# A chunked state-space scan on one core: broadcast decays and exponentials loaded per chunk, tanh written over the taps' input

## The chip, the core and the metric

The kernel runs on one core of one Trainium2 chip. The metric is the device time of one execution in microseconds (us); the median of three executions of the kernel before is 2815.06 us.

## What is computed

Two pre-norm residual layers run over 1024 tokens of width 1024, batch 1, in float32: a mixer of mLSTM and retention heads, an MLP, a second mixer (Mamba-2 SSD) and another MLP. The change touches the second mixer alone. It has 32 heads of 64 in 8 groups of 4, state size 128, a causal depthwise convolution of 4 taps, and chunks of 128 tokens. What it computes, cut to what matters here:

```python
zxbcdt = u @ w_in
z, xbc, dt = jnp.split(zxbcdt, (SSD_INNER, SSD_INNER + SSD_CONV_DIM), axis=-1)
xbc = jax.nn.silu(causal_depthwise_conv(xbc, conv_w, conv_b).astype(F32))
xs, bm, cm = jnp.split(xbc, (SSD_INNER, SSD_INNER + SSD_GROUPS * SSD_STATE), axis=-1)
dt = jax.nn.softplus(dt.astype(F32) + dt_bias.astype(F32))
cs = jnp.cumsum(dt * a.reshape(ng, rep), axis=2)            # inside a chunk
seg = jnp.exp(jnp.where(mask, cs[:, :, :, None] - cs[:, :, None, :], -jnp.inf))
cb = jnp.einsum('bctgn,bcsgn->bctsg', cm, bm)
m = cb[..., None] * seg * dt[:, :, None]
y_intra = jnp.einsum('bctsgr,bcsgrp->bctgrp', m, x)
states = jnp.einsum('bclgn,bclgr,bclgrp->bcgrpn', bm, to_end, x)
h_c = exp(cs[:, :, -1]) * h_{c-1} + states                  # from chunk to chunk
y_inter = jnp.einsum('bctgn,bcgrpn->bctgrp', cm, h_prev) * jnp.exp(cs)[..., None]
y = y_intra + y_inter + d_skip * xs
yg = y * silu(z);  yg = group_rmsnorm(yg) * norm_w;  out = yg @ w_out
```

## The kernel before, in words

Tokens lie along the free dimension and channels on the partitions; a half is 512 tokens. Every float32 weight is split into a high and a low part (`split`, L92 to L95: ScalarE writes `whi`, VectorE subtracts to get `wlo`), and a projection of 128 columns for one half (`proj_in`, L136) is 24 matmuls of 512 columns into one PSUM bank.

The second mixer (`ssd`) goes over 8 groups of heads. First `ssd_dt` computes the cumulated log-decays and their exponentials for all tokens and stores them in DRAM as `cs_d` and `ecs_d`, one row per head. In each group then:

- **Projection and taps.** Four column blocks (B, C and two of x) are projected, 2 halves each. ScalarE copies the PSUM bank into `xr` (L769) and writes the last tap into `sact` (L770), VectorE adds three more taps (L774), ScalarE takes the tanh (L778, into a tile `th`), and VectorE finishes the SiLU (L779).
- **Scan.** 8 chunks, 4 in each half. For each half `cbp` (L801) is the product of B and C, masked into `cb`. For each chunk the log-decays of the group's four heads, 4 x 128 numbers, are loaded from `cs_d` and broadcast over 128 partitions into `cb4` (L812, 256 KB written; the profile calls the tile `cb`). ScalarE makes the decay matrix of them: four Relu instructions, one per head (L816), and one Exp (L823). VectorE multiplies by `cb` (L824). TensorE transposes x and B (`tr`, L829); VectorE scales x into `xd` and `xw` (L832, L852), ScalarE copies the transposed B into `bn` (L856). TensorE computes the chunk's own part and the part from the state, both into one PSUM tile `yp` (L838, L843), and the new state's contribution `ds_` (L858), which needs `bn` and `xw`. VectorE adds it to the state, which GpSimd has multiplied by the chunk's decay. The part from the state is multiplied by the broadcast exponentials `eh` (L872) and added (L883). `eh` is loaded per half, for 4 heads by 64 partitions each, in 4 transfers of 128 KB (L793).
- **Gate and output.** Two column blocks of z are projected (L136), gated and squared (L893 to L909); a matmul with ones, `sp` (L914), sums the squares; the output projection (L180) follows.

The program's text is written in this order, but a scheduler sets the order on each engine: it interleaves the z projection's 96 matmuls with the scan's small steps, and moves instructions ahead where it estimates that their inputs are there. Each engine runs its queue strictly in order. Of the z matmuls stand, between the `tr` of a chunk and its `yp`, in the second group and the ones after it: before 18, 4, 10, 10, 9, 8, 16 and 9 for chunks 0 to 7, 4 between `yp` and `ds_` of chunk 0, and 8 after the last chunk. Loads are all issued by the SP queue. `cb4` has 2 buffers before, so that the load of chunk c+2 waits for the matmuls L838 of chunk c; the loads for the next group's first two chunks are issued in the scan of this one.

Of the kernel before, what the change touches and what calls it, by code (L numbers as in the profile page):

```python
# [7 lines left out]
F32 = mybir.dt.float32  # L8
# [4 lines left out]
P = 128  # L13
# [4 lines left out]
HALF = 512  # L18
# [5 lines left out]
class Trunk:  # L24
# [694 lines left out]
    def ssd(self, w_in, conv_w, conv_b, dt_bias, a_log, d_skip, norm_w, w_out, mask):  # L719
        nc, tc = self.nc, self.tc  # L720
        with ExitStack() as ctx:
            one = ctx.enter_context(tc.tile_pool(name="ss1", bufs=1))
            two = ctx.enter_context(tc.tile_pool(name="ss2", bufs=2))
# [27 lines left out]
            nat, cs_d, ecs_d, dec, by_token = self.ssd_dt(one, w_in, dt_bias, a_log)  # L751


            for g in range(8):
                conv = []
                for j in (2, 3, 0, 1):
                    jt = (g * 2, g * 2 + 1, 16 + g, 24 + g)[j]
                    w = self.split_in(self.load_in(w_in, 2048 + jt * P))
                    outs = []
                    prev = None  # L760
                    for half in range(2):
                        ps = self.proj_in(w, half)
                        t = self.half_tile(half, f"sact{half}")
                        xr = two.tile([P, HALF + 3], F32, name="xr", tag="xr", bufs=3)
                        if half == 0:
                            nc.gpsimd.memset(xr[:, 0:3], 0.0)
                        else:
                            nc.gpsimd.tensor_copy(xr[:, 0:3], prev[:, HALF : HALF + 3])
                        nc.scalar.copy(xr[:, 3 : 3 + HALF], ps)  # L769
                        nc.scalar.activation(  # L770
                            t, ps, AF.Identity, scale=cw[:, 3, jt : jt + 1], bias=cw[:, 4, jt : jt + 1]
                        )
                        for k in range(3):
                            nc.vector.scalar_tensor_tensor(  # L774
                                t, xr[:, k : k + HALF], cw[:, k, jt : jt + 1], t, op0=ALU.mult, op1=ALU.add
                            )
                        th = two.tile([P, HALF], F32, name="th", tag="th", bufs=2)
                        nc.scalar.activation(th, t, AF.Tanh)  # L778
                        nc.vector.scalar_tensor_tensor(t, th, 1.0, t, op0=ALU.add, op1=ALU.mult)  # L779
                        outs.append(t)  # L780
                        prev = xr
                    conv.append(outs)
# [3 lines left out]
                hs = slice(g * 4, g * 4 + 4)  # L786
                state = None
                for half in range(2):
                    o = half * HALF
                    eh = two.tile([P, 2, HALF], F32, name="eh", tag="eh", bufs=1)  # L790
                    for tl in range(2):
                        for j in range(2):
                            nc.sync.dma_start(  # L793
                                eh[j * 64 : (j + 1) * 64, tl],
                                ecs_d[g * 4 + tl * 2 + j, o : o + HALF].partition_broadcast(64),
                            )

                    cbp = self.sc.tile([P, CPH, P], F32, name="cbp", tag="sc")
                    for cc in range(CPH):
                        s = slice(cc * P, (cc + 1) * P)  # L800
# [5 lines left out]
                    y = (x0[half], x1[half])  # L806
                    for cc in range(CPH):
                        c = half * CPH + cc
                        s = slice(cc * P, (cc + 1) * P)
                        par, q = c % 2, c // 2  # L810
                        cb4 = two.tile([P, 4, P], F32, name="cb4", tag="cb4", bufs=2)
                        nc.sync.dma_start(  # L812
                            cb4, cs_d[hs, c * P : (c + 1) * P].partition_broadcast(P)
                        )
                        for h in range(4):
                            nc.scalar.activation(  # L816
                                cb4[:, h],
                                cb4[:, h],
                                AF.Relu,
                                scale=-1.0,  # L820
                                bias=nat[:, 2, par, g * 4 + h, q : q + 1],
                            )
                        nc.scalar.activation(cb4, cb4, AF.Exp, scale=-1.0)  # L823
                        nc.vector.tensor_mul(  # L824
                            cb4, cb4, cb[:, cc].unsqueeze(1).broadcast_to([P, 4, P])
                        )
                        tr = self.sc.tile([P, 4, P], F32, name="tr", tag="sc")
                        for j, src in enumerate((x0, x1, bT)):
                            nc.tensor.transpose(tr[:, j], src[half][:, s], self.ident)  # L829
                        xn = tr[:, 0:2].rearrange("p a (h d) -> p (a h) d", h=2)  # L830
                        xd = two.tile([P, 4, 64], F32, name="xd", tag="xd")
                        nc.vector.tensor_mul(  # L832
                            xd, xn, nat[:, 0, par, hs, q : q + 1].broadcast_to([P, 4, 64])
                        )
                        yp = self.sc.tile([P, 4, P], F32, name="yp", tag="sc")
                        for h in range(4):
                            r = slice((h % 2) * 64, (h % 2) * 64 + 64)
                            nc.tensor.matmul(  # L838
                                yp[r, h // 2], xd[:, h], cb4[:, h], start=True, stop=True
                            )  # L840
                        if c > 0:
                            for tl in range(2):
                                nc.tensor.matmul(  # L843
                                    yp[:, 2 + tl],
                                    state[:, tl * P : (tl + 1) * P],
                                    cT[half][:, s],
                                    start=True,
                                    stop=True,
                                )
                        if c < NCH - 1:  # L850
                            xw = two.tile([P, 4, 64], F32, name="xw", tag="xw")
                            nc.vector.tensor_mul(  # L852
                                xw, xn, nat[:, 1, par, hs, q : q + 1].broadcast_to([P, 4, 64])
                            )
                            bn = two.tile([P, P], F32, name="bn", tag="bn")
                            nc.scalar.copy(bn, tr[:, 2])  # L856
                            ds_ = self.sc.tile([P, HALF], F32, name="ds_", tag="sc")
                            nc.tensor.matmul(  # L858
                                ds_[:, 0:256], bn, xw.rearrange("p h d -> p (h d)"), start=True, stop=True
                            )  # L860
                            new = two.tile([P, 256], F32, name="sst", tag="sst")
                            if c == 0:
                                nc.scalar.copy(new, ds_[:, 0:256])
                            else:
                                nc.gpsimd.tensor_mul(
                                    new.rearrange("p (h d) -> p h d", h=4),
                                    state.rearrange("p (h d) -> p h d", h=4),
                                    dec[:, hs, c : c + 1].broadcast_to([P, 4, 64]),
                                )
                                nc.vector.tensor_add(new, new, ds_[:, 0:256])  # L870
                        if c > 0:
                            nc.vector.tensor_mul(eh[:, :, s], eh[:, :, s], yp[:, 2:4])  # L872
                        for tl in range(2):
                            nc.vector.scalar_tensor_tensor(
                                y[tl][:, s],
                                y[tl][:, s],
                                dsk[:, g * 2 + tl : g * 2 + tl + 1],
                                yp[:, tl],
                                op0=ALU.mult,
                                op1=ALU.add,  # L880
                            )
                            if c > 0:
                                nc.vector.tensor_add(y[tl][:, s], y[tl][:, s], eh[:, tl, s])  # L883
                        if c < NCH - 1:
                            state = new
                zs = []
                for j in range(2):
                    w = self.split_in(self.load_in(w_in, g * 256 + j * P))
                    outs = []
                    for half in range(2):  # L890
                        ps = self.proj_in(w, half)
                        t = self.z_tile("sz")
# [5 lines left out]
                for half in range(2):  # L898
                    hid = self.hid_tiles()
                    y = (x0[half], x1[half])  # L900
# [200 lines left out]
```

## Time and profile before

| | |
|---|---|
| median of 3 executions | 2815.06 us (2813.73 to 2817.12) |
| the profiled execution's own time | 2813.8 us |
| its span, first to last instruction | 2812.0 us |
| mean granted TensorE clock | 0.993 of full speed |
| TensorE matmuls (PE) busy | 2735.5 us, 97% |
| VectorE (DVE) busy | 1696.3 us, 60% |
| ScalarE (ACT) busy | 933.9 us, 33% |
| GpSimd (POOL) busy | 500.3 us, 18% |
| chain that ended last, by engine | PE 91%, DMA 4%, ACT 2%, DVE 2%, POOL 1% |

Busy times are of the whole span, which has stages with different limits; the second mixer takes the stretch from about 1203 to 2112 us. Its eight scans lie some 114 us apart. A busy matmul row tells that one was in the engine, not that it ran at its peak. The waiting time of an engine costs only where the engine that bounds the stage is held up in turn. The chain goes back from the last instruction, at each step to what released it.

### The profile page before, as it was taken

The numbers are of one execution on the slowest core, as the hardware profiler recorded it, in microseconds if no ns is written. First come the engines' busy times: TensorE is split into PE (matmuls) and PEld (weight loads), VectorE is DVE, ScalarE is ACT, GpSimd is POOL, SyncE is SP. The second block draws the span as 40 slices with busy tenths as digits, with TensorE's granted clock in tenths as the row PEclk, the third lists the DMA queues.
The fourth block names the chain that finished last, engine by engine and source line by source line (L and its number), as shares of the span: only waits on it lengthen the run. The fifth ranks groups of instructions, "written<-read, shape, count | busy, mean of one in ns | idle before, by whom it ended". The sixth has DMA issues, their size and how long they took to land.

```text
span 2812.0 us, 33165 instructions
## 1 busy us (share of the span) xinstructions
PE 2735.5 (97%) x13149; PEld 2206.2 (78%) x13149; DVE 1696.3 (60%) x2794; ACT 933.9 (33%) x1547; POOL 500.3 (18%) x454
## 2 busy tenths in 40 slices
PE   8999999999999999899999999999999999999997
PEld 7788787888888888687787777777778888888885
DVE  5544436645656445876667667666676566654457
ACT  5131223322222222443433434344344222222223
POOL 1000000322233222300000000000013222322223
PEclk9999999999999999899999999999999999999999
DMA  4021210211111111032212222122221111110111
GB/s 157 23 77 31 60 53 23 68 45 60 60 60 46 37 39 55 23 81 74 67 54 70 67 67 75 51 70 68 59 62 53 60 60 60 53 42 27 60 38 60
DMA packets 199050, 161.47 MB, mean 57 GB/s; under 512 B 8952, under 2 KB 177840, under 8 KB 198768
## 3 DMA queue, kind: packets, MB, share of 16 engines
q1 hardware_dynamic: 198896, 159.36, 19.3%
q8 instruction: 103, 1.69, 0.2%
q14 instruction: 51, 0.42, 0.0%
HBM read 154.68 MB, written 4.62 MB: 57 GB/s over the span
## 4 chain that ended last, share of the span: by engine, by line
PE 91%; DMA 4%; ACT 2%; DVE 2%; POOL 1%; issue 0%; SPq 0%; DVEq 0%; ACTq 0%; POOLq 0%
PE mmin L136 49%; PE mmout L260 21%; PE mmout L180 9%; DMA cb<-cs_d 4%; PE mmnat L152 3%; PE yp L838 1%; PE pt L223 1%; PE bank L536 1%; PE bank L540 1%; ACT cb L816 1%; POOL h L355 1%; DVE un L206 1%; PE dc L548 1%; PE mmin L162 1%; PE cbp L801 1%; PE bank L508 0%
## 5 line engine op out<-in xcount | busy, mean ns | idle before, releaser
L136 PE MATMUL mmin<-uh,whi 128*128 128x512 f32 (+1 forms) x2112 | 825.6, 391 | 0.3 <-ACT uh L225 0.3
L136 PE MATMUL mmin<-ul,whi 128*128 128x512 f32 (+1 forms) x2112 | 825.9, 391 | 0.0
L136 PE MATMUL mmin<-uh,wlo 128*128 128x512 f32 (+1 forms) x2112 | 822.3, 389 | 0.0
L136 PEld LDWEIGHTS mmin<-uh,whi 128*128 128x128 f32 x2112 | 397.3, 188 | 90.8 <-issue 1.2
L136 PEld LDWEIGHTS mmin<-uh,wlo 128*128 128x128 f32 x2112 | 397.6, 188 | 88.0 <-issue 0.2
L136 PEld LDWEIGHTS mmin<-ul,whi 128*128 128x128 f32 x2112 | 397.6, 188 | 86.9
L94 DVE TENSOR_TENSOR wlo<-raw,whi 128x1024 fp32r<-128x1024 f32 x240 | 309.8, 1294 | 222.8 <-ACT whi L93 220.0
L93 ACT CAST whi<-raw 128x1024 fp32r<-128x1024 f32 (+1 forms) x243 | 251.1, 1038 | 461.0 <-PE mmin L136 220.4
L260 PE MATMUL mmout<-whi,hl 128*128 128x512 f32 x896 | 354.0, 395 | 0.7 <-DVE hl L94 0.7
L260 PE MATMUL mmout<-wlo,hh 128*128 128x512 f32 x896 | 353.9, 395 | 0.0
L260 PE MATMUL mmout<-whi,hh 128*128 128x512 f32 x896 | 353.9, 395 | 0.0
L180 PE MATMUL mmout<-whi,hid 128*128 128x512 f32 x768 | 245.5, 398 | 0.8 <-ACT hid L600 0.8
L311 DVE TENSOR_TENSOR q<-q 128x512 f32<-128x512 f32 x128 | 95.2, 744 | 221.9 <-ACT q L310 221.9
L283 DVE TENSOR_TENSOR h<-h,mmout 128x512 f32<-128x512 f32 x320 | 208.9, 679 | 33.2 <-PE mmout L260 33.0
L260 PEld LDWEIGHTS mmout<-whi,hl 128*128 128x128 f32 x896 | 168.7, 188 | 40.8 <-DVE hl L94 1.1
L260 PEld LDWEIGHTS mmout<-wlo,hh 128*128 128x128 f32 x896 | 168.7, 188 | 39.7
L260 PEld LDWEIGHTS mmout<-whi,hh 128*128 128x128 f32 x896 | 168.7, 188 | 39.8
L774 DVE SCALAR_TENSOR_TENSOR sact<-xr,cw,sact 128x512 f32<-128x512 f32 x192 | 144.2, 751 | 56.0 <-ACT sact L770 51.6
L180 PEld LDWEIGHTS mmout<-whi,hid 128*128 128x128 f32 x768 | 143.5, 188 | 36.1 <-ACT hid L600 2.5
L310 ACT ACTIVATE q<-mmin 128x512 f32<-128x512 f32 x128 | 76.3, 596 | 269.6 <-PE mmin L136 269.6
L180 PE MATMUL mmout<-wlo,hid 128*128 128x512 f32 x384 | 150.2, 395 | 0.0
L93 ACT CAST hh<-q 128x1024 fp32r<-128x1024 f32 x80 | 84.1, 1051 | 198.8 <-PE mmout L260 110.0
(374 smaller groups left out, 3178.8 us busy)
## 6 DMA issues: line engine op xcount, KB each, us to landing
raw<-in_mlp_w_dram SPq DMA_DIRECT2D x64, 512.0 KB
raw<-in_mlp_w_dram SPq DMA_DIRECT2D x32, 1024.0 KB
raw<-in_ssd_w_in_dram SPq DMA_DIRECT2D x48, 512.0 KB
cb<-cs_d SPq DMA_DIRECT2D x64, 256.0 KB
raw<-in_hyb_w_in_dram SPq DMA_DIRECT2D x24, 512.0 KB
raw<-in_ssd_w_out_dram SPq DMA_DIRECT2D x16, 512.0 KB
eh<-ecs_d SPq DMA_DIRECT2D x64, 128.0 KB
h<-in_x_dram SPq DMA_DIRECT2D x8, 512.0 KB
```

What stands on the lines that cost most here:

```text
L93: self.nc.scalar.copy(hi, raw)
L94: self.nc.vector.tensor_sub(lo, raw, hi.bitcast(F32))
L136: self.nc.tensor.matmul(ps[:, o : o + n], a[:, k], u[:, k, s], start=(k == 0 and i == 0), stop=(k == 7 and i == 2),)
L152: self.nc.tensor.matmul(ps, u[:, k, s], a, start=(k == 0 and i == 0), stop=(k == 7 and i == 2))
L162: self.nc.tensor.matmul(ps, w[:, k], u[:, k, s], start=(k == 0 and i == 0), stop=(k == 7 and i == 1))
L180: self.nc.tensor.matmul(ps, a[:, s], w[:, n], start=(kk == 0 and i == 0), stop=(kk == 1 and i == 2))
L206: nc.vector.scalar_tensor_tensor(un[j], self.h[:, c, n], r, wb[j], op0=ALU.mult, op1=ALU.mult)
L260: nc.tensor.matmul(banks[t], a[x][:, kk, s], w[y][:, kk], start=(not more and kk == 0 and i == 0), stop=(not more and kk == 1 and i == 2), ...
L283: nc.vector.tensor_add(y, y, x[t])
L310: nc.scalar.activation(x, ps, AF.Relu)
L311: nc.vector.tensor_mul(x, x, x)
L774: nc.vector.scalar_tensor_tensor(t, xr[:, k : k + HALF], cw[:, k, jt : jt + 1], t, op0=ALU.mult, op1=ALU.add)
```

## The change

It does three things in `ssd`: the tanh is written into the first 512 columns of `xr`, so that the tile `th` (two buffers of 2 KB per partition) is gone; `cb4` gets 4 buffers instead of 2; and `eh` is loaded per chunk, in two transfers of 64 partitions by 2 x 128 numbers (64 KB each), into 4 buffers, and not at all for chunk 0, which has no state before it.

```diff
-                        th = two.tile([P, HALF], F32, name="th", tag="th", bufs=2)
+
+                        th = xr[:, 0:HALF]
                         nc.scalar.activation(th, t, AF.Tanh)
...
-                    o = half * HALF
-                    eh = two.tile([P, 2, HALF], F32, name="eh", tag="eh", bufs=1)
-                    for tl in range(2):
-                        for j in range(2):
-                            nc.sync.dma_start(
-                                eh[j * 64 : (j + 1) * 64, tl],
-                                ecs_d[g * 4 + tl * 2 + j, o : o + HALF].partition_broadcast(64),
-                            )
...
-                        cb4 = two.tile([P, 4, P], F32, name="cb4", tag="cb4", bufs=2)
+                        cb4 = two.tile([P, 4, P], F32, name="cb4", tag="cb4", bufs=4)
                         nc.sync.dma_start(
                             cb4, cs_d[hs, c * P : (c + 1) * P].partition_broadcast(P)
                         )
+                        if c > 0:
+                            eh = two.tile([P, 2, P], F32, name="eh", tag="eh", bufs=4)
+                            for j in range(2):
+                                nc.sync.dma_start(
+                                    eh[j * 64 : (j + 1) * 64],
+                                    ecs_d[hs, c * P : (c + 1) * P]
+                                    .rearrange("(a b) t -> b a t", b=2)[j]
+                                    .partition_broadcast(64),
+                                )
...
-                            nc.vector.tensor_mul(eh[:, :, s], eh[:, :, s], yp[:, 2:4])
+                            nc.vector.tensor_mul(eh, eh, yp[:, 2:4])
...
-                                nc.vector.tensor_add(y[tl][:, s], y[tl][:, s], eh[:, tl, s])
+                                nc.vector.tensor_add(y[tl][:, s], y[tl][:, s], eh[:, tl])
```

The scheduler makes new orders of it. From L815 on, line numbers of the changed kernel are 2 higher (Relu is L818, Exp L825, `bn` L858). Below, a tile's number tells its chunk: in the second group `cb_10434`, `cb_10469`, `cb_10516`, `cb_10551`, `cb_10586` and `cb_10621` are chunks 2 to 7 before, and `cb_11279` and `cb_11308` the next group's chunks 0 and 1. After the change `cb_10510`, `cb_10548`, `cb_10586` and `cb_10624` are chunks 4 to 7, and `cb_11272`, `cb_11301`, `cb_11339` and `cb_11377` the next group's chunks 0 to 3. The copies `bn` follow each other by chunk, from 0 to 6.

ScalarE's queue in the first half of the second group's scan, before, from the state copy of chunk 0:

```order
L863 COPY sst<-ds__10393 128x256
L893 ACTIVATE sz<-mmin 128x512
L816 ACTIVATE cb_10434<-cb_10434,dnat 128x128
L856 COPY bn<-tr 128x128
L816 ACTIVATE cb_10434<-cb_10434,dnat 128x128 x3
L823 ACTIVATE cb_10434<-cb_10434 128x512
L816 ACTIVATE cb_10469<-cb_10469,dnat 128x128 x4
L856 COPY bn<-tr 128x128
L823 ACTIVATE cb_10469<-cb_10469 128x512
L816 ACTIVATE cb_10516<-cb_10516,dnat 128x128 x4
L856 COPY bn<-tr 128x128
```

The `bn` here are those of chunks 1, 2 and 3, each behind a Relu of the chunk that is one ahead. The same place after the change:

```order
L865 COPY sst<-ds__10383 128x256
L895 ACTIVATE sz<-mmin 128x512
L818 ACTIVATE cb_10510<-cb_10510,dnat 128x128
L858 COPY bn<-tr 128x128
L818 ACTIVATE cb_10510<-cb_10510,dnat 128x128 x3
L825 ACTIVATE cb_10510<-cb_10510 128x512
L818 ACTIVATE cb_10548<-cb_10548,dnat 128x128 x4
L858 COPY bn<-tr 128x128
L825 ACTIVATE cb_10548<-cb_10548 128x512
L818 ACTIVATE cb_10586<-cb_10586,dnat 128x128 x3
L858 COPY bn<-tr 128x128
```

The `bn` of chunks 1, 2 and 3 now stand behind Relus of chunks 4, 5 and 6, whose loads wait for `yp` of chunks 0, 1 and 2.

ScalarE's queue in the second half of the same scan, before, from the Relus of chunk 5:

```order
L816 ACTIVATE cb_10551<-cb_10551,dnat 128x128 x4
L856 COPY bn<-tr 128x128
L823 ACTIVATE cb_10551<-cb_10551 128x512
L893 ACTIVATE sz<-mmin 128x512
L903 ACTIVATE sact_10233<-sz 128x512
L908 ACTIVATE hid_10783<-sz,snw 128x512
L856 COPY bn<-tr 128x128
L816 ACTIVATE cb_10586<-cb_10586,dnat 128x128 x4
...
L816 ACTIVATE cb_11279<-cb_11279,dnat 128x128 x4
L903 ACTIVATE sact_10311<-sz 128x512
L908 ACTIVATE hid_10784<-sz,snw 128x512
```

The second `bn` is chunk 5's, ahead of the next Relu; the second square (L903) stands behind the next group's chunk 0, whose load waits for `yp` of chunk 6. After the change, from the Relus of the next group's chunk 0:

```order
L818 ACTIVATE cb_11272<-cb_11272,dnat 128x128 x4
L858 COPY bn<-tr 128x128
L825 ACTIVATE cb_11272<-cb_11272 128x512
L818 ACTIVATE cb_11301<-cb_11301,dnat 128x128 x4
L858 COPY bn<-tr 128x128
L825 ACTIVATE cb_11301<-cb_11301 128x512
L905 ACTIVATE sact_10232<-sz 128x512
L910 ACTIVATE hid_10789<-sz,snw 128x512
L895 ACTIVATE sz<-mmin 128x512
L818 ACTIVATE cb_11339<-cb_11339,dnat 128x128 x4
L825 ACTIVATE cb_11339<-cb_11339 128x512
L818 ACTIVATE cb_11377<-cb_11377,dnat 128x128
L905 ACTIVATE sact_10308<-sz 128x512
```

The first `bn` is chunk 5's, now behind the next group's chunk 0 (its load waits for `yp` of chunk 4); the second square stands behind the next group's chunk 3, whose load waits for `yp` of chunk 7. The last group has no such Relus.

SP's queue in the same scan after the change:

```order
L805 DMA cb_10586<-cs_d 128x4x128
L811 DMA eh<-ecs_d 64x2x128 x2
L805 DMA cb_10624<-cs_d 128x4x128
L811 DMA eh<-ecs_d 64x2x128 x2
L805 DMA cb_11272<-cs_d 128x4x128
L811 DMA eh<-ecs_d 64x2x128 x2
L805 DMA cb_11301<-cs_d 128x4x128
L811 DMA eh<-ecs_d 64x2x128 x2
L805 DMA cb_11339<-cs_d 128x4x128
L70 DMA raw<-in_ssd_w_in_dram 128x8x128
L811 DMA eh<-ecs_d 64x2x128 x2
L805 DMA cb_11377<-cs_d 128x4x128
```

Between two loads of decays now go two of exponentials, where before four larger ones went together once in a half. On TensorE the order of kinds is the same; the z matmuls between `tr` and `yp` of chunks 0 to 7 are now 18, 4, 9, 7, 9, 9, 10 and 11, and 15 follow the last chunk.

## Rows read from the trace of the kernel before

**Rows 1.** Busy time per stretch: between two scans, and the sum over eight scans.

```profile
1292.00:1360.00 68.00, 68.00 (x302) 55.12 (x302) 43.79 (x59) 23.89 (x37) 3.30 (x10) 1.00 0.20 56
...
sum 366.00, PE 332.10 PEld 255.98 DVE 271.07 ACT 181.56 POOL 33.87; mean PE 41.51 PEld 32.00 DVE 33.88 ACT 22.70 POOL 4.23
```

The columns of rows 1: stretch and length in us, busy PE, PEld, DVE, ACT and POOL (with instructions), granted clock, DMA share, GB/s.

**Rows 2.** Waits of ScalarE in the second mixer: total us, times, longest.

```profile
ACT cb L816 <- DMA cb<-cs_d: 118.4, 53, 5.4
```

**Rows 3.** Timeline of PE, second group: start, duration, instruction, [idle before <- releaser].

```profile
1371.94 0.70 PE L858 MATMUL ds__10424<-xw,bn 128*128 128x256 f32 x2 [1.34 <-ACT bn L856]
...
1382.73 0.70 PE L858 MATMUL ds__10494<-xw,bn 128*128 128x256 f32 x2 [1.81 <-ACT bn L856]
...
1397.09 0.66 PE L838 MATMUL yp<-cb,xd 128*64 128x128 f32 x8 [0.76 <-DVE xd L832]
...
1399.12 0.70 PE L858 MATMUL ds__10611<-xw,bn 128*128 128x256 f32 x2 [0.73 <-ACT bn L856]
```

**Rows 4.** The chain of waits through the second group: start, us, what.

```profile
1366.59 4.72 DMA cb<-cs_d
...
1371.34 0.40 ACT cb L816
1371.74 0.16 ACT bn L856
...
1381.56 0.97 ACT cb L816 x3
...
1383.43 0.89 PE cbp L801 x8
1384.32 0.33 PE tr L829 x3
1384.65 2.10 PE mmin L136 x9
1386.75 0.59 PE yp L838 x8
1387.34 0.64 PE yp L843 x4
1387.98 0.43 PE ds__10541 L858 x2
...
1396.64 1.28 ACT cb L816 x4
...
1405.82 0.82 PE sp L914 x8
```

**Rows 5.** Timeline of SP's issues and of ScalarE, second group: exponentials ahead of decays.

```profile
1385.27 2.37 SPq L793 DMA_DIRECT2D eh<-ecs_d  x4
1387.75 0.52 SPq L812 DMA_DIRECT2D cb<-cs_d  x1
...
1393.94 1.28 ACT L816 ACTIVATE cb<-cb,dnat 128x128 f32<-128x128 f32 x4 [3.37 <-DMA cb<-cs_d]
```

**Rows 6.** The chain over all eight groups: shortest and longest of 23 loads.

```profile
1263.61 4.48 DMA cb<-cs_d
...
1730.35 6.40 DMA cb<-cs_d
```

**Rows 7.** Timeline of VectorE and ScalarE, second group: an addition, square and sum.

```profile
1378.75 0.28 DVE L883 TENSOR_TENSOR sact<-sact,eh 128x128 f32<-128x128 f32 x1
...
1403.76 0.62 ACT L903 ACTIVATE sact<-sz 128x512 f32<-128x512 f32 x1
...
1404.78 0.69 DVE L904 TENSOR_TENSOR sact<-sact,sact 128x512 f32<-128x512 f32 x1
```

**Rows 8.** Timeline of PE, fifth group; busy time per stretch after stalls, two groups.

```profile
1739.31 0.70 PE L858 MATMUL ds__13338<-xw,bn 128*128 128x256 f32 x2 [2.35 <-ACT bn L856]
...
1739.98:1743.38 3.40, 3.40 (x12) 2.73 (x11) 3.11 (x9) 2.19 (x6) 0.00 (x0) 0.50 0.05 12
...
1951.60:1955.00 3.40, 2.89 (x11) 2.71 (x12) 0.88 (x3) 0.99 (x4) 0.62 (x1) 0.50 0.12 30
```

## The prediction

> **What bounds the kernel now.** Read the busy time per stretch first: in a stretch between two scans TensorE is busy the whole time, 68.00 of 68.00 us, and over the eight stretches in which the second mixer scans its chunks it is busy 332.1 of 366 us [rows 1]. TensorE bounds the kernel, and all that this change can reach is those 33.9 us of idle scan time, 4.2 us in each of 8 groups. The list of ScalarE's waits says what lies behind: 118.4 us in 53 waits for the broadcast load of the decays [rows 2]. Most of that costs nothing, since TensorE has z-projection matmuls to run. The timeline of one group shows what does cost: four stalls, 1.34, 1.81, 0.76 and 0.73 us, 4.64 in all [rows 3]. The chain shows why: a load lands 4.72 us after issue, ScalarE does its first Relu on it (0.40), then the copy `bn` (0.16), and only then can TensorE start `ds_` [rows 4]. `bn` itself waits for nothing: it stands behind a Relu that waits for the load, on a queue that runs in order.
>
> **The change, part by part.** *The tanh.* ScalarE writes it over the taps' input: same instruction, same size, no time. An `xr` buffer is held until the addition after the tanh; it is needed again three half-projections later, 3 x 24 matmuls of 0.233 us (2.10 for 9) [rows 4] = 16.8 us, so I cost that at nothing.
>
> *The exponentials.* 64 loads of 128 KB become 112 of 64 KB, and the multiplication and addition keep their size. Four issues took 2.37 us of SP [rows 5], so 48 more are 28 us over 8 groups on a queue that mostly waits. No engine waits for them: each is issued four chunks ahead. What they can do is delay a load of decays behind them. Before, with four of them (512 KB) just ahead, a load issued at 1387.75 was usable at 1393.94, 6.2 us [rows 5].
>
> *The decays.* Four buffers instead of two look as if the wait should go. The orders shown above say otherwise. ScalarE now does Relu and Exp four chunks ahead too: in the second group, behind the `bn` of chunk 0, it has the Relu of chunk 4, whose load can only go out when the first matmuls of `yp` of chunk 0 have freed the buffer. This is the same moment at which chunk 2's load went out before, and `bn` of chunk 1 stands right behind that Relu, as before. The prefetch is spent on ScalarE's order, and does not become slack. VectorE's multiplications by `cb` move ahead with it; VectorE is busy 271 of the 366 us of scans [rows 1], and in the walk below none of its results is the last to arrive, except the sum of squares, which is counted.
>
> So I walk the second group on the trace's clock. Durations are those of the chain [rows 4]: `tr` 0.33, `yp` 0.59 and 0.64, `ds_` 0.43 (0.70 after a stall), `cbp` 0.89, a projection matmul 0.233. Relu is 0.40 for one, 0.97 for three, 1.28 for four, `bn` 0.16, and 0.1 for hand-overs. A load takes 4.95 us from issue to landing: the mean of the chain's 23 pieces, which lie between 4.48 and 6.40 [rows 6].
> - Up to `ds_` of chunk 1 at 1371.94 nothing differs: stall 1.34.
> - Chunk 2: 1371.94 + 0.70 + 0.33 + 9 matmuls 2.10 = 1375.07; `yp` frees its buffer at 1375.66 and ends at 1376.30. The load for chunk 5 went out as before; `bn` is ready, no stall.
> - Chunk 3: + 0.43 + 0.33 + 7 matmuls 1.63 + 1.23 = 1379.92. `bn` stands behind three Relus of chunk 6: 1375.66 + 4.95 + 0.97 + 0.16 + 0.1 = 1381.84. Stall 1.9 (before 1.81).
> - Chunk 4: + 0.70 + 0.89 + 0.33 + 2.10 + 1.23 = 1387.1. Chunk 7's load, free to go at 1379.3, stands on SP behind exponentials that wait for VectorE's addition of chunk 2, which before ended at 1379.03 [rows 7] and here ends about 1378.9; two issues of 0.6 take them to 1380.1, and `bn` is ready at 1387.1. No stall, and no room either. The other exponentials get out before the `yp` that the load behind them needs.
> - Chunk 5: + 0.43 + 0.33 + 2.10 + 1.23 = 1391.15. `bn` now stands behind the four Relus of the next group's chunk 0, loaded from 1386.4: 1386.4 + 4.95 + 1.28 + 0.16 + 0.1 = 1392.9. Stall 1.75; before, this `bn` stood ahead of the next Relu.
> - Chunks 6 and 7 fit by 0.5 us and more: the 0.76 and 0.73 are gone. `yp` of chunk 7 frees its buffer at 1401.4.
> - The sum over squares, `sp`: TensorE is there at 1402.05 + 17 matmuls 3.96 (two of the output projection) = 1406.0. It needs the second square, which now stands behind a Relu of the next group's chunk 3: 1401.4 + 4.95 + 0.40 + 0.62 + 0.69 + 0.1 = 1408.2 [rows 4, 7]. Stall 2.15, against none: before, the Relu ahead of that square belonged to a load that had gone out a chunk earlier, and the square ran at 1403.76 [rows 7].
>
> Sum 7.15 against 4.64 us, and `sp` at 1408.2 instead of 1405.82: +2.4 us a group. In the last group no next group is loaded, so only 1.34 + 1.9 remain: -1.4. 7 x 2.4 - 1.4 = **+15.4**.
>
> Two more terms. Exponentials now pass between the loads; 128 KB a chunk is a quarter of the 512 KB that added 6.2 - 4.95 = 1.25 us, so 0.3 on each of three stalls in 7 groups: **+6.6** with the last group's one. And the clock: before, after a stall of 2.35 us, TensorE was granted 0.50 (1.2 GHz) for 3.40 us [rows 8]; half of 3.40 is 1.7 us lost. It happened in two of the eight scans, and no stall shorter than 2.35 us was followed by it. Two go (-3.4). Of 21 stalls near 2.0 to 2.5 I expect a quarter to bring it: 5.5 x 1.7 = +9.4; net **+6**. In the first group eight exponentials and two more loads queue ahead of three weight loads: ten issues, some 6 us by [rows 5], is the upper bound, 0 the lower; I take 0, as those weights are needed only after the scan.
>
> 15.4 + 6.6 + 6 = +28. The sum is made against the profiled execution, 2813.8 us (span 2812.0), 1.3 under the median of 2815.06: **2842 us**.
>
> Bounds: with every load at 4.48 us, no exponentials in the way and no half clock, the three loaded stalls shrink by 0.47 each: 7 x 1.0 - 1.9 - 3.4 = +2, 2816. With 6.40 us each they grow by 1.45: 7 x 6.8 + 36 - 3.4 = +80, 2894, where 36 is 21 half-clock spells. I stay near the mean of the 23 pieces, which is nearer to their low end.
>
> **Rivals.** *Faster: the depth pays.* If loads land well before the Relu, all four stalls go with their two half clocks: 2813.8 - 33.9 - 3.4 = 2776; with half of it, 2795. For it speaks that 118 us of ScalarE's waiting is for just these loads; against it, that the queue lets the Relu come as soon as its buffer is freed, so that a load's whole time is waited for. It decides where a load takes about 4.1 us: there the three stalls fall by 0.84 each and the sum equals the old one; below 2.8 nothing is left of them. No piece is under 4.48 [rows 6]. This is what the Trainium skill promises in "DMA: Bandwidth & Descriptors", section "Rules for kernel authors": issue the DMA early, compute, wait on its semaphore late. Its section "Anatomy of one DMA" puts a DMA on GpSimd's path at about 2.0 us plus bytes over 436 GB/s, an estimate of 2.6 us for 256 KB, by which every stall would be gone and the time 2776; these loads go out on SP, and the rows' 4.72 us and more decide against it.
>
> *No change.* Loads no longer behind a burst of four exponentials land at the low end, 4.5 us, and no half clock appears: 2811 to 2820.
>
> *Slower still.* Each of the 21 stalls brings a half clock: 21 x 1.7 - 9.4 = +26, 2868. Against it: the 1.81 us stall did not.
>
> *The change does not do what it says.* The loads are issued on the release of the buffer four chunks back, so it does; but that ScalarE's order follows them is the forecast itself.
>
> **How the numbers follow.** About 0.2% is what a measurement of this kernel can tell from no change; that is 5.6 us. Slower by more: 0.74, my forecast with the still slower case (0.10 of it). No change: 0.14. Faster: 0.12. The forecast's own range is 2816 to 2894. For 8 in 10 I go from 2813, leaving out the faster case, to 2868, the clock's case.
>
> **What would show it.** Right: in the changed profile TensorE's idle scan time is 50 to 70 us; the waits on `bn` sit at `ds_` of chunks 1, 3 and 5; a new wait of about 2 us at `sp` is released by DVE or ScalarE; `yp` no longer waits for `xd`; ScalarE's waiting for decays stays above 80 us; 0.50 clock appears in more scans. Wrong: a load in the chain under 4 us, `ds_` of chunk 5 without a wait, or `sp` starting at once.

## The result and the profile after

| | before | changed |
|---|---|---|
| median of 4 executions | 2815.26 us | 2863.89 us (2861.73 to 2869.21) |
| span of the profiled execution | 2812.0 us | 2859.9 us |
| idle of TensorE in the second mixer | 33.9 us | 63.2 us |
| TensorE busy in the second mixer | 875.6 us | 893.8 us |

The changed kernel is slower: 1.0175 times the time before, 95% interval 1.0158 to 1.0193. The 47.9 us of span, save 0.4, lie in the second mixer, as the busy time per stretch shows. The columns are those of [rows 1]. First the mixer before, then after:

```profile
1203.00:2112.50 909.50, 875.60 (x4417) 698.48 (x4416) 629.35 (x1160) 378.15 (x755) 63.03 (x131) 1.00 0.25 67
```

```profile
1203.00:2160.00 957.00, 893.80 (x4424) 708.90 (x4423) 627.86 (x1159) 376.78 (x755) 60.58 (x131) 0.98 0.25 62
```

The idle time grew by 63.2 - 33.9 = 29.3 us. Busy time grew by 18.2 us although the instructions are the same: the mean granted clock fell to 0.98. Idle time and clock are thus two terms of nearly known size.

The timeline of TensorE in the second group of the changed kernel, all its stalls over 0.1 us, answers to [rows 3]:

```profile
1381.68 0.70 PE L860 MATMUL ds__10417<-xw,bn 128*128 128x256 f32 x2 [1.35 <-ACT bn L858]
...
1392.01 0.70 PE L860 MATMUL ds__10493<-xw,bn 128*128 128x256 f32 x2 [2.03 <-ACT bn L858]
...
1404.60 0.70 PE L860 MATMUL ds__10576<-xw,bn 128*128 128x256 f32 x2 [1.67 <-ACT bn L858]
...
1409.35 0.70 PE L860 MATMUL ds__10614<-xw,bn 128*128 128x256 f32 x2 [0.16 <-ACT bn L858]
...
1422.44 1.84 PE L916 MATMUL sp<-ones,sact 128*128 128x1 f32 x8 [4.29 <-DVE sact L906]
```

They sit at `ds_` of chunks 1, 3, 5 and 6 and at the sum of squares; `yp` has none. The lists of waits give the sums over the mixer, for TensorE at the sum of squares and for ScalarE at the decays (118.4 us before, [rows 2]):

```profile
PE sp L916 <- DVE sact L906: 21.9, 7, 4.3
```

```profile
ACT cb L818 <- DMA cb<-cs_d: 157.7, 57, 5.4
```

So twice the buffers brought ScalarE more waiting for the same loads. The chain through the second group shows the two that end last there:

```profile
1402.36 5.43 DMA cb<-cs_d
...
1408.18 0.97 ACT cb L818 x3
...
1409.35 0.70 PE ds__10614 L860 x2
...
1413.67 6.89 DMA cb<-cs_d
...
1421.60 0.70 DVE sact L906
...
1422.44 1.84 PE sp L916 x8
```

The load that ends at 1420.56 is that of the next group's chunk 3. This group does not need it; it needs the square that stands behind its Relu. SP's issues show what stood ahead of it:

```profile
1409.85 0.38 SPq L70 DMA_DIRECT2D raw<-in_ssd_w_in_dram  x1
1411.85 1.73 SPq L811 DMA_DIRECT2D eh<-ecs_d  x2
1413.67 0.55 SPq L805 DMA_DIRECT2D cb<-cs_d  x1
```

A weight load of 512 KB went out 3.8 us ahead and two of exponentials right ahead. That these made it 6.89 us long is likely but not shown: in the first group, where no weight load goes out in the 5 us before it, the same load took 4.79 us, but no run takes the weight load away. And the clock behind such a stall, by busy time per stretch, in the fifth group (3.40 us) and the second (6.80 us, part of it the stall's end):

```profile
1785.85:1789.25 3.40, 3.40 (x9) 2.61 (x9) 1.24 (x3) 1.88 (x5) 0.87 (x1) 0.50 0.00 0
1421.30:1428.10 6.80, 5.66 (x19) 4.88 (x20) 3.47 (x6) 4.96 (x10) 1.38 (x1) 0.55 0.00 0
```

Nine matmuls in 3.40 us at 0.50 (1.2 GHz), as in [rows 8].

### The profile page after: what moved, and what is told of

Same layout as the page of the kernel before. It is cut to its first block, busy times and chain, and to the rows that moved or that the text cites. A ratio compares the mean times of both kernels' runs of the same rounds, so it can differ in the third digit from the quotient of the medians.

```text
span 2859.9 us, 33251 instructions
## 1 busy us (share of the span) xinstructions
PE 2755.7 (96%) x13149; PEld 2217.4 (78%) x13149; DVE 1694.9 (59%) x2794; ACT 932.7 (33%) x1547; POOL 498.8 (17%) x454
## 4 chain that ended last, share of the span: by engine, by line
PE 89%; DMA 6%; ACT 2%; DVE 2%; POOL 1%; issue 0%; SPq 0%; DVEq 0%; ACTq 0%; POOLq 0%
PE mmin L136 48%; PE mmout L260 21%; PE mmout L180 9%; DMA cb<-cs_d 6%; PE mmnat L152 3%; ACT cb L818 1%; PE yp L840 1%; PE pt L223 1%; PE bank L536 1%; PE bank L540 1%; POOL h L355 1%; PE mmin L162 1%; DVE un L206 1%; PE dc L548 1%; PE sp L916 1%; PE tr L831 0%
## 5 line engine op out<-in xcount | busy, mean ns | idle before, releaser
L180 PE MATMUL mmout<-whi,hid 128*128 128x512 f32 x768 | 253.1, 409 | 0.8 <-ACT hid L600 0.8
```

The source lines that it names most:

```text
L180: self.nc.tensor.matmul(ps, a[:, s], w[:, n], start=(kk == 0 and i == 0), stop=(kk == 1 and i == 2))
```

## The experiments

Theory A is the prediction's: ScalarE's order puts `bn` and the second square behind Relus whose loads go out late. Rivals: the loads of exponentials between the decays cost the time (B); the buffers pay, given the right order (C); the tanh's place costs (D).

**One part of the change at a time.** `depth_alone` is the kernel before with

```diff
-                        th = two.tile([P, HALF], F32, name="th", tag="th", bufs=2)
+                        th = xr[:, 0:HALF]
...
-                        cb4 = two.tile([P, 4, P], F32, name="cb4", tag="cb4", bufs=2)
+                        cb4 = two.tile([P, 4, P], F32, name="cb4", tag="cb4", bufs=4)
```

> The kernel before with four buffers of decays and the tanh written over the taps' input; the exponentials stay four large loads per half. Theory A (ScalarE's order: bn and the second square stand behind Relus whose loads go out late): most of the loss is here, since ScalarE's order again has the Relus of the chunk four ahead in front of bn of chunks 1, 2, 3 and 6, and the next group's chunk 3 in front of the second square. Idle of 1.3 and 1.8 us at ds_ of chunks 1 and 3 and of 2 to 4 us at the sum of squares in seven groups, each of the latter followed by half clock: 2830 to 2850 us. Theory B (the loads of exponentials between the loads of decays cost the time): they are as before, so 2800 to 2818 us.

Measured 2846.26 us, 1.0115 times before (1.0094 to 1.0135). The wait at the sum of squares is there with the exponentials as before, which speaks against B as the whole cause:

```profile
PE sp L914 <- DVE sact L904: 17.3, 7, 3.2
```

Only five of these seven waits were followed by half clock, where each was expected to be.

`exps_alone` is the changed kernel with `bufs=2` for `cb4`.

> The changed kernel with two buffers of decays instead of four: exponentials per chunk and the tanh over the input stay. Theory A: the second square stands behind a Relu of the next group's chunk 0 only, as before, so there is no wait at the sum of squares; the waits at ds_ of chunks 1 and 3 stay as before and one more may come in the second half: 2810 to 2832 us. Theory B: the exponentials still pass between the decays, so most of the loss stays: 2840 to 2865 us.

Measured 2834.79 us, 1.0068 (1.0049 to 1.0088), 3 us beyond A's range. There is no wait at the sum of squares, but one of 4.9 us in all, in seven groups, right ahead of it at the output projection, which needs ScalarE's scaling of the gate. The second group's stalls of 0.7 us and more, by the timeline of TensorE:

```profile
1380.89 0.70 PE L860 MATMUL ds__10417<-xw,bn 128*128 128x256 f32 x2 [1.40 <-ACT bn L858]
...
1391.67 0.70 PE L860 MATMUL ds__10493<-xw,bn 128*128 128x256 f32 x2 [1.87 <-ACT bn L858]
...
1403.80 0.70 PE L860 MATMUL ds__10576<-xw,bn 128*128 128x256 f32 x2 [1.61 <-ACT bn L858]
```

The third is the "one more" that the expectation allowed for. ScalarE's timeline has `bn` of chunk 5 behind the Relus and the Exp of chunk 6, which wait for their load; before, this `bn` stood ahead of them:

```profile
1401.66 1.28 ACT L818 ACTIVATE cb<-cb,dnat 128x128 f32<-128x128 f32 x4 [3.27 <-DMA cb<-cs_d]
1402.97 0.63 ACT L825 ACTIVATE cb<-cb 128x512 f32<-128x512 f32 x1
1403.50 0.25 ACT L858 COPY bn<-tr 128x128 f32<-128x128 f32 x1
```

So the split of the exponentials costs here too, but again through `bn`'s place. Nine stretches of half clock, against two before, are part of the loss.

`tanh_alone` is the kernel before with the first of those edits alone.

> The kernel before with the tanh written over the taps' input and nothing else. Theory A: same instruction, same size, an input buffer held a little longer than needed elsewhere: no change, 2808 to 2820 us. Theory D (the longer hold of the input delays a projection's bank or the taps): over 2822 us, with waits of ScalarE's copy into the input ahead of the scans.

Measured 2813.29 us, 0.9995 (0.9985 to 1.0004): nothing, as costed. D falls.

**The order alone.** `order_bn` is the changed kernel with an edge: a rule for the scheduler that one instruction is queued behind another, here on ScalarE. Nothing waits for anything more.

```diff
+            mark = None
             for g in range(8):
...
-                        for h in range(4):
-                            nc.scalar.activation(
+                        with tc.issue_after(mark) if mark is not None else ExitStack():
+                            for h in range(4):
+                                nc.scalar.activation(
...
-                            nc.scalar.copy(bn, tr[:, 2])
+                            mark = nc.scalar.copy(bn, tr[:, 2]).ins
```

(The Exp stands in the block too.)

> The changed kernel with an order edge on ScalarE alone: the Relus and the Exp of a chunk may not be issued ahead of the copy bn of the chunk before it. Loads, buffers and sizes are those of the changed kernel. Theory A: bn never stands behind a Relu that waits for a late load, loads have three chunks (some 15 us) to land, and the idle of TensorE in the scans falls from 63 us to under 8, with no half clock: 2776 to 2790 us, faster than both kernels. Theory B: the loads are still delayed by the exponentials: 2830 to 2865 us.

Measured 2770.92 us, 0.9847 (0.9832 to 0.9861): 43 us faster than before and 93 faster than the changed kernel, 5 us under the range, with the same loads and buffers. In the mixer TensorE is busy 868.61 of 869 us at full clock:

```profile
1203.00:2072.00 869.00, 868.61 (x4436) 696.00 (x4435) 630.12 (x1160) 378.41 (x759) 60.62 (x130) 1.00 0.27 69
```

On ScalarE's timeline no Relu waits for a load any more; `bn` comes first, and where it waits it is released by VectorE's `xw` of the same chunk, which `ds_` needs too:

```profile
1372.68 0.27 ACT L860 COPY bn<-tr 128x128 f32<-128x128 f32 x1 [3.09 <-DVE xw L856]
1372.84 1.28 ACT L820 ACTIVATE cb<-cb,dnat 128x128 f32<-128x128 f32 x4
1374.15 0.64 ACT L827 ACTIVATE cb<-cb 128x512 f32<-128x512 f32 x1
```

B falls: the exponentials still go between the decays, and the loads were early enough for their own chunk all the time; the order threw it away. But the scheduler planned the other engines anew as well. From the second group on, the z matmuls between `tr` and `yp` of chunks 0 to 7 are now 18, 8, 10, 10, 12, 12, 12 and 10, with none after the last chunk, and VectorE's multiplications by the masked `cb` come later. So `order_bn` alone does not show that all 93 us are ScalarE's order; the next two runs change less.

**The two places apart.** `sq_order` is the changed kernel with that block, but the mark is set at the gate's scaling instead of at `bn`:

```diff
-                        nc.scalar.mul(hid[0][j], zt, w1)
+                        mark = nc.scalar.mul(hid[0][j], zt, w1).ins
```

> The changed kernel with an order edge that keeps only the Relus of the next group behind this group's gate work (squares and scaling on ScalarE); inside a group Relus still run four chunks ahead of bn. Theory A: the waits at the sum of squares (21.9 us in seven groups) and the seven half clocks behind them go, and with them the waits at ds_ of chunk 5, whose bn stood behind the next group's chunk 0; ds_ of chunks 1 and 3 keep theirs, 1.35 and 1.8 us: 2812 to 2832 us. Theory B (loads slow in themselves): under 10 us of gain, 2850 to 2865 us.

Measured 2807.39 us, 0.9973 (0.9962 to 0.9985), 56 us under the changed kernel and 5 below the range. TensorE has its kinds of instructions in exactly the order of the changed kernel, in all groups, so this gain is not one of moved matmuls. What is left is `ds_` of chunks 1 and 3, two stalls in each of eight groups, as in these rows of TensorE's timeline:

```profile
1373.51 0.70 PE L862 MATMUL ds__10417<-xw,bn 128*128 128x256 f32 x2 [1.29 <-ACT bn L860]
...
1383.16 0.70 PE L862 MATMUL ds__10493<-xw,bn 128*128 128x256 f32 x2 [1.46 <-ACT bn L860]
```

`bn_vector` does the reverse: the squares stay where they were, and VectorE copies `bn`.

```diff
-                            nc.scalar.copy(bn, tr[:, 2])
+                            nc.vector.tensor_copy(bn, tr[:, 2])
```

> The changed kernel with bn copied by VectorE instead of ScalarE, no order edge. Theory A: the waits at ds_ (about 41 us) go, those at the sum of squares stay at 2 to 4 us with a half clock behind each: 2795 to 2822 us. Theory B: the loads are late whoever copies bn, and the waits move to yp, which needs the decays themselves: 2840 to 2865 us.

Measured 2819.5 us, 1.0019 (1.001 to 1.0028). The waits at `ds_` are gone, also at chunk 3, which from the second group on has seven z matmuls ahead of its `yp` as in the changed kernel. TensorE's list of waits in the mixer has one entry over 1 us: ScalarE's gate work behind the same Relu, met at the output projection, four of whose matmuls here stand ahead of the sum of squares. The busy time shows the clock:

```profile
PE mmout L180 <- ACT hid L910: 23.5, 7, 3.7
```

```profile
1203.00:2114.00 911.00, 887.52 (x4427) 709.40 (x4426) 636.79 (x1217) 371.35 (x701) 60.86 (x131) 0.98 0.26 65
```

This prices one such stall. Busy time is 887.5 - 868.6 = 18.9 us above that of `order_bn`, with VectorE's copies hidden: seven stalls of 3.4 us cost 23.5 us of waiting and 2.7 us each of half clock on top. Taken singly, the two places bring 56.5 us (`sq_order`) and 44.4 us (`bn_vector`); together, in `order_bn`, 93.0.

**What each part is worth once the order is right.** `order_two` is the kernel before with the edge alone; `order_depth` is `depth_alone` with the edge; `order_chunk2` is `exps_alone` with the edge.

> The kernel before (two buffers of decays, exponentials per half, its own tile for the tanh) with nothing but the same order edge on ScalarE: no Relu or Exp of a chunk ahead of bn of the chunk before it. Theory A (order alone): a load then has from the first matmuls of yp of chunk c to those of chunk c+2, two rounds of about 4.1 us, for 4.95 us of loading, 1.28 of Relus, 0.6 of Exp and 0.6 of the multiplication, 7.5 us in all: it fits by some 0.7 us, save where the load stands behind four exponentials (6.2 us): 2772 to 2790 us. Theory C (the four buffers are what pays once the order is right): waits for the decays come back at yp in most chunks, and it stays within 10 us of the kernel before: 2803 to 2818 us.

> Four buffers of decays, the tanh over the input and the order edge, but the exponentials in four large loads per half as before. Theory A: as with exponentials per chunk, no idle in the scans: 2768 to 2776 us. If the exponentials per chunk are themselves worth something once the order is right, this is slower than the 2770.9 us by more than its interval; if they are a burden, faster.

> Two buffers of decays, exponentials per chunk, the tanh over the input and the order edge: the fourth corner beside 2800.7 (two buffers, per half), 2786.4 (four, per half) and 2770.9 us (four, per chunk). If the two parts of the change help each by itself once the order is right, about 2785 us, 2778 to 2792. If a load that goes out on the release two chunks back also has two issues of exponentials of 0.6 us ahead of it on SP, the 0.7 us of room is used up and waits come at yp: 2792 to 2812 us.

| buffers of decays | exponentials | no edge | with edge |
|---|---|---|---|
| 2 | per half | 2814 (before) | 2800.68, ratio 0.9951 (0.9931 to 0.997) |
| 2 | per chunk | 2834.79 | 2775.26, ratio 0.9858 (0.9845 to 0.9871) |
| 4 | per half | 2846.26 | 2786.38, ratio 0.9898 (0.9881 to 0.9916) |
| 4 | per chunk | 2863.89 | 2770.92, ratio 0.9847 (0.9832 to 0.9861) |

In the left column both parts make it slower, in the right one both make it faster: whether the change is good or bad hangs on the order that comes with the edge. TensorE's order of kinds is the same in `order_two` and `order_depth`, and another one in both `order_chunk2` and `order_bn`; so with the edge the two depths are compared on one order, the two ways of loading exponentials are not. `order_two` came out 11 us above A's range and 2 below C's, between the two, and `order_depth` 10 above its own. Their waits say why, TensorE's in `order_two` and then in `order_depth`:

```profile
PE yp L840 <- DVE xd L834: 13.1, 13, 2.1
PE mmout L180 <- ACT hid L910: 7.9, 7, 1.2
```

```profile
PE yp L840 <- DVE xd L834: 10.2, 7, 1.9
```

With four buffers the decays are early, so the wait has another source. It is the four loads of exponentials for a half, which can only go out when the one buffer is free. VectorE's timeline and SP's issues in the second group of `order_depth`:

```profile
1390.37 0.42 DVE L874 TENSOR_TENSOR eh<-eh,yp 128x256 f32<-128x256 f32 x1 [2.30 <-DMA eh<-ecs_d]
```

```profile
1382.40 2.37 SPq L794 DMA_DIRECT2D eh<-ecs_d  x4
```

Issued from 1382.40 on, usable at 1390.37: VectorE stands 2.30 us, its next `xd` comes late, and `yp` of chunk 6 with it. Per chunk this is gone. How much of the 15 us between `order_depth` and `order_bn` it is worth stays open: `order_depth` also has five z matmuls fewer ahead of `yp` of chunks 5 and 6 (8 and 11 against 12 and 12), some 1.2 us a group by [rows 4], an estimate, and `eh` has one buffer there against four of a quarter of the size. Per chunk, two buffers of decays nearly do: TensorE waits 3.2 us at `yp` in the whole mixer, and two more buffers bring 4.3 us by the medians, with intervals of the ratios that overlap. `order_chunk2` came out 3 us under the range of its first reading; the second, issues of exponentials eating the room, did not come.

## Why the prediction was right, and where its sum was small

- **Direction and mechanism: right.** Stalls were worked out for the second group as 1.34, 1.9 and 1.75 at `ds_` of chunks 1, 3 and 5, and measured 1.35, 2.03 and 1.67. `yp` no longer waits for `xd`, the new wait at `sp` is there, and ScalarE's waiting for decays rose instead of falling. `sq_order` confirms the cause at `sp` with TensorE's order unchanged, and `bn_vector` confirms it at `ds_`; `order_bn` does away with both.
- **The tanh and 48 more issues: right**, 2813.29 us against 2814.96 for the first; of the first group's 6 us of delayed weights nothing came (TensorE is busy all the time from the first group's gate to the next scan).
- **The idle time: 29.3 us where 15.4 + 6.6 = 22 stood.** Two pieces were mis-sized. At `sp` the forecast was 2.15 and 0.3 for exponentials, 2.45 a group; measured 21.9 / 7 = 3.1. The load of the next group's chunk 3 was taken at the mean of 4.95 us, though a weight load and a pair of exponentials stand just ahead of it on SP; it took 6.89 in the second group and 5.5 to 6.0 in the five after it. That is 4.7 us. And chunk 6 was said to fit "by 0.5 us and more": its `ds_` waited 0.16 to 1.05 us in six groups, 3.8 in all, as the loads ahead took 5.4 to 6.3 us. Two more errors pull against each other: `ds_` of chunks 1, 3 and 5 waited 36.8 us in all groups, where the prediction's stalls, each loaded one with its 0.3 for exponentials, make 42.7; and the groups of the kernel before have 33.9 us of idle time, not eight times the second group's 4.64, which is 37.1. That so little of them shows in the sum is luck.
- **The clock: 18.2 us where 6 stood**, the larger miss. The step that failed was "a quarter" of 21 stalls. All ten stalls of 2.03 us and more were followed by half clock, one twice as long, eleven spells of about 1.7 us; less the two of before, 9 x 1.7 = 15.3. The other 2.9 us of busy time are not assigned. Seven of the ten are at `sp`, so the mis-sized wait there may also have set off the clock; that is not shown. The rival "slower still" (2868) came nearest by luck: ten of the stalls brought half clock, not 21, and more idle time made up the rest.
- **Not settled:** which stalls bring half clock (below).

The depth-pays rival was right in one thing: with ScalarE free of the wait for loads, all idle time goes (0.4 us are left). Its bound of 2776 us was even passed (2770.9). The Trainium skill's rule in "DMA: Bandwidth & Descriptors", "Rules for kernel authors", to issue early and wait late, is what `order_bn` does (2770.9 us); the changed kernel issued early and then waited early (2863.9 us), on a queue with other work behind. The same section of the Trainium skill says to coalesce many small transfers into one large one. Here, with the edge, 64 KB pieces in place of bursts of four of 128 KB went with 2775.3 us against 2800.7, which the rule would not lead one to expect. When the piece needed first can go out is the likely reason, by the 2.30 us wait above; but the number of buffers and TensorE's order changed with the size of the pieces, and no run keeps these apart.

## What to carry to other kernels

More buffers move the loads earlier, but a scheduler may use them to move the consumers earlier on an in-order engine; then the engine waits for the new loads in front of work that others need now. Read the order of the waiting engine before counting a prefetch as slack, and ask of each waiting instruction what stands behind it. Here an edge that holds the consumer back turned a loss of 49 us into a gain of 43. Since a scheduler may plan every engine anew for one edge, compare the other engines' orders too before the gain is put down to the edge alone.

## What the hardware showed that was not expected

Stalls of 2 to 4 us can cost more than their length. In `bn_vector` TensorE ran 18.9 us longer for seven of them. Yet length alone does not decide: in the changed kernel none of 1.84 us or less was followed by half clock, while in `exps_alone` one of 1.62 us was (0.55 over the 3.40 us behind it), and in `depth_alone` two of 2.21 and 2.37 us were not. What else decides, these runs do not show. These are the stretches behind those three, `exps_alone` first:

```profile
1984.60:1988.00 3.40, 3.34 (x10) 2.70 (x11) 3.40 (x10) 0.40 (x2) 0.62 (x1) 0.55 0.24 51
```

```profile
1774.10:1777.50 3.40, 3.31 (x19) 2.90 (x20) 2.50 (x5) 3.37 (x8) 1.42 (x1) 1.00 0.00 0
1657.92:1661.32 3.40, 3.40 (x19) 2.94 (x20) 2.50 (x5) 3.37 (x8) 1.41 (x1) 1.00 0.00 0
```
